# Later expert rows, a longer lag for their second-table products, and fewer of them beside the gate tables

## The chip, the cores and the metric

The kernel runs on one core of a Trainium2 chip. The metric is the device time of one execution in microseconds, less is better; a time is the median of several executions. The engines are named as the profile names them: PE (TensorE, matrix products), DVE (VectorE), ACT (ScalarE), POOL (GpSimd, which here issues the indirect gathers) and SP (which issues plain DMAs).

## What is computed

One decoder layer over 1024 prompt tokens and 8 sample tokens. Three mixers (a state-space scan, a convolution, attention to a memory) are summed and normed; behind them stands a feed-forward step that picks 128 experts for each token out of 16384 (8 heads, 16 each) and costs this case its gathers:

```python
# t: tokens x 1024; idx, gate: tokens x 8 heads x 16 picks, from two top-16 lists of 128 keys
u = jnp.take(u_tab, idx, axis=0)
act = jax.nn.gelu(jnp.einsum('td,thkd->thk', t, u), approximate=False)
v = jnp.take(v_tab, idx, axis=0)
return jnp.einsum('thk,thkd->td', gate * act, v)
# then x <- layer_norm(ALPHA * x + that)
```

Both tables are 16384 x 1024 in float32, so one row of either is 4 KB.

## The kernel before

The prompt is worked in three groups of 256, 384 and 384 tokens, one after the other on PE; the 8 sample tokens ride along. Each group passes the mixers (`front`, `main`), a norm (`norm1`) and the routing, which finds the experts (`routing`, `route`).

**Expert rows.** For the first two groups, five blocks of 128 tokens, the experts are gathered. A "row" is one pick for 128 tokens: one gather of 128 x 4 KB by POOL (`gather`, L442) into one of `UVB` = 8 buffers named `uv`, and the arithmetic on it. In the first table (`block_u`) that is one DVE multiplication whose sum goes into a column of `av` (L455), 128 rows to a block. The second table has two forms. `block_v` gathers strips by `ixt` and lets PE multiply and sum: four rows make a set, and `four(m, vs)` issues the set's eight matmuls (L501). `block_v2` (`second_table`, L544), used once the third group's mixers are done (`strips` is false), gathers by `idx` and does each row with one DVE multiply and add; PE has no part in it. At a block's end stand `layer_norm2` (L436, L439) and the store.

**What sets the pace.** `product`, which every matrix product with a streamed weight calls, first calls `spread`. That adds `pace[0]` (a pair, for first-table and second-table rows) to two counters `due` and issues as many rows as are due. `pace[0]` is taken from `PHASES` in the mixers, from `PACE[-3]` from L1409 on (the third group's norm, its routing and its gate tables), from `PACE[-2]` in the first 24 rounds of the dense loop, and from `PACE[-1]` behind them. The products of a complete set wait in the list `late` until `VLAG` more rows are out, so that the gathers have time to land; a finished block's step to its second table waits there `TLAG` rows.

**What sets the order.** The program text is only the first order. A scheduler then gives each engine its list: of what can be issued it takes the instruction with the lowest number, which is the place in the text. Rows are issued inside `tc.issue_after(last)` (behind the fourth-last DVE instruction that is no row, `LAG`) and `tc.high_priority(-LATER)`, which adds `LATER` to their numbers. The products in `late` get no such number.

**The third group.** Its 384 tokens take no rows: `dense_group` computes all 16384 experts. First, for all tokens, gate tables are made: one-hot products (L1314) go through ACT to tiles `xt` and to DRAM (`gd`, 16 stores, L1321), while 30 of the 128 blocks of activations are computed ahead (`activations`, PE lines L200 and L211) and stored in `ad`. Then `while active` waits for a block of `block_v` in progress, whose last step (L522) reads the accumulators `va`, since the dense loop needs them. The dense loop has 128 rounds: activations of six rounds ahead (read back from `ad` in the first 24, computed behind them), a DVE product with the gates (`weigh`, L1346, tiles read back from `gd`, L1340), and 18 matmuls (L1378). Its layer norms follow (L1382 to L1388), then `while more()` issues the rows that are left, and `sample_final` (L1271, L1272) ends the program. The sample tokens have a state update of their own (L1058 on PE, L1061 on ACT, L1066 to L1075), scheduled between the products of the second group.

Of the kernel before, what the change touches and what calls it, by code (L numbers as in the profile page):

```python
# [37 lines left out]
    ((0, 0),) * 6,  # L38
    ((1.7, 2), (1.8, 1.8), (1.8, 1.8), (2.2, 1.8), (1.4, 1.8), (2.4, 1.8)),
    ((1.4, 2), (1.8, 1.8), (1.8, 1.8), (2.2, 1.8), (1.4, 1.8), (2.4, 1.8))))  # L40
PACE = (1.5, 2.0), (1.0, 1.0), (2.2, 2.2)
LAG = 4
RIDE = 0
LATER = 1000000
PRE = 6
EARLY = 30
STEP = 4
VLAG = 6
TLAG = 10
E2B = 7  # L50
BLKB = 28
# [17 lines left out]
def hybrid_layer(ctx: ExitStack, tc, I, O):  # L69
# [193 lines left out]
    def row(work):  # L263
        while work:
            try:
                next(work[0])
                return
            except StopIteration:
                work.popleft()

    def spread():
# [9 lines left out]
        while max(due) >= 1.0 or (late and not any(tables) and steps < 4):  # L281
# [8 lines left out]
            n = len(nc.cur_bb.bb.instructions)  # L290
            with tc.issue_after(last), tc.high_priority(-LATER):
                row(tables[k])
# [187 lines left out]
    def block_v(g, c, idx, av, avt, ixt):  # L480
# [8 lines left out]
        def four(m, vs):  # L489
            if m == 0:  # L490
                va.extend(pva() for _ in range(2))
            w = slide[m % 2]
            act.activation(w[:, :, 31], avt[:, m:P:32], AF.Copy)

            before = None
            for dh in range(2):
                for j in (3, 0, 1, 2):
                    with ExitStack() as order:
                        if before is not None:
                            order.enter_context(tc.issue_after(before))  # L500
                        before = pe.matmul(va[dh][32 * j:32 * j + 32], w[:, j, 31 - m:63 - m],  # L501
                                           vs[j][:, dh * 512:dh * 512 + 512], start=(m == 0), stop=(m == 31)).ins

        for m in range(32):
            vs = []
            for j in range(4):
# [3 lines left out]
                if j < 3:  # L510
                    yield
            late.append([VLAG, lambda m=m, vs=vs: four(m, vs)])
            yield
        done = []
        late.append([VLAG, lambda: done.append(1)])
        while not done:
# [297 lines left out]
    def norm1(G):  # L814

        g, nt, tb = G.g, G.nt, G.tb
        rs_ = G.rs
        layer_norm_f(rs_, nt)
        for f in range(8):
            act.activation(rs_[f], rs_[f], AF.Identity, scale=col(C_G1, f), bias=col(C_B1, f))  # L820

    def keep_tokens(G):

        for c in range(G.tb):
            for i in range(4):
                pt = psm()
                for f in range(2):
                    pe.transpose(pt[:, f * P:(f + 1) * P], G.rs[2 * i + f][:, c * P:(c + 1) * P], ident)
                xt = blk(256)
                act.activation(xt, pt[:, 0:256], AF.Copy)  # L830
                sp.dma_start(x1d[G.g][c][:, i * 256:(i + 1) * 256], xt)
# [446 lines left out]
    def dense_group(G):  # L1278
# [73 lines left out]
        for c in range(P):  # L1352
            if c + PRE < P:
                if c == 2 * EARLY:
                    keep_tokens(G)
                pace[0] = PACE[-2 if c + PRE < early else -1]
                if c + PRE < early:
# [50 lines left out]
    sp.dma_start(O["state"], hT)  # L1408
    pace[0] = PACE[-3]  # L1409
    norm1(G)  # L1410
# [104 lines left out]
```

## Time and profile before

| | us |
|---|---|
| median of 3 runs (4582.04 to 4594.18) | 4582.82 |
| profiled execution | 4586.19 |
| its span, first to last instruction | 4584.4 |
| PE busy | 3917.6 (85%) |
| DVE busy | 3294.7 (72%) |
| ACT busy | 1755.5 (38%) |
| POOL busy | 1633.8 (36%) |

The third group's routing runs from some 3000 to 3190 us, its gate tables to 3445 us, the dense loop from 3470 to 4540 us, and the tail to 4584.4 us. All rows below are from the profiled execution, whose time is 1.8 us above its span and 3.4 us above the median.

### The profile page before, as it was taken

How to read it: one execution, taken by the hardware profiler on the slowest of the kernel's cores; microseconds unless marked ns; L12 is line 12 of the kernel's file. 1: busy time of each engine (PE TensorE's matmuls, PEld its weight loads, DVE VectorE, ACT ScalarE, POOL GpSimd, SP SyncE). 2: the span in 40 equal slices, each digit the busy share in tenths (PEclk: the TensorE clock that was granted, in tenths of full speed). 3: DMA queues.
4: the chain of work that ended last, by engine and by line, in shares of the span. 5: the costliest groups of instructions: out<-in, count | busy, mean ns of one | idle time of the engine just before them, and what ended most of it. 6: DMA issues, size and time to landing. Idle time of an engine off the chain costs nothing. (4 is left out here: it accounts for less than half of the span.)

```text
span 4584.4 us, 58298 instructions
## 1 busy us (share of the span) xinstructions
PE 3917.6 (85%) x19901; PEld 3043.3 (66%) x19901; DVE 3294.7 (72%) x7235; ACT 1755.5 (38%) x3699; POOL 1633.8 (36%) x1316
## 2 busy tenths in 40 slices
PE   8999898798488888885888888888996999889996
PEld 8888786576377556563666665444664788777895
DVE  4458537775799746776766886458896889888976
ACT  5474243546334314342362322112563333332333
POOL 0000000341422456512444535534322556547631
PEclk9999999898799999997999999999997999999998
DMA  5433344653866899954888879967879999999985
GB/s 173 150 129 132 120 148 155 230 208 110 287 228 225 290 372 344 340 189 144 287 291 317 319 248 332 352 227 258 305 284 321 350 374 389 352 318 295 386 297 188
DMA packets 410041, 1199.41 MB, mean 262 GB/s; under 512 B 42464, under 2 KB 111712, under 8 KB 407568
## 3 DMA queue, kind: packets, MB, share of 16 engines
q0 software_dynamic: 186880, 679.56, 41.7%
q1 hardware_dynamic: 222864, 516.13, 32.4%
q8 instruction: 157, 2.57, 0.2%
q14 instruction: 140, 1.15, 0.1%
HBM read 1141.59 MB, written 53.93 MB: 261 GB/s over the span
## 5 line engine op out<-in xcount | busy, mean ns | idle before, releaser
L442 POOL DMA_INDIRECT uv<-in_peer_u,idx x640 | 794.6, 1242 | 1846.5 <-DVE idx L422 800.9
L200 PE MATMUL mm<-xt,wh 128*128 128x384 f32 (+1 forms) x4224 | 1042.5, 332 | 45.4 <-ACT b L921 28.7
L455 DVE SCALAR_TENSOR_TENSOR uv<-uv,x 128x1024 f32<-128x1024 f32 x640 | 774.0, 1218 | 365.3 <-DMA uv<-in_peer_u,idx 322.8
L200 PEld LDWEIGHTS mm<-xt,wh 128*128 128x128 f32 x4224 | 742.4, 192 | 102.9 <-issue 31.1
L211 PE MATMUL mm<-b,wr 128*128 128x256 f32 (+2 forms) x2304 | 723.5, 466 | 73.6 <-ACT b L737 43.6
L200 PE MATMUL mm<-xt,wl 128*128 128x384 f32 (+1 forms) x2112 | 687.5, 326 | 36.2 <-DVE wl L191 36.0
L189 ACT ACTIVATE wh<-wr 128x1024 fp32r<-128x1024 f32 x362 | 383.1, 1059 | 851.9 <-PE mm L200 371.8
L442 POOL DMA_INDIRECT uv<-in_peer_v,ixt x384 | 437.9, 1140 | 666.8 <-PE va L501 223.8
L211 PEld LDWEIGHTS mm<-b,wr 128*128 128x128 f32 x2304 | 436.2, 195 | 319.2 <-ACT b L737 53.8
L191 DVE TENSOR_TENSOR wl<-wr,wh 128x1024 fp32r<-128x1024 f32 x362 | 441.2, 1219 | 268.4 <-ACT wh L189 263.8
L442 POOL DMA_INDIRECT uv<-in_peer_v,idx x256 | 352.3, 1376 | 340.4 <-DVE uv L544 174.8
L200 PEld LDWEIGHTS mm<-xt,wl 128*128 128x128 f32 x2112 | 404.5, 192 | 51.9 <-DVE wl L191 41.7
L678 DVE SCALAR_TENSOR_TENSOR b<-raw,cc,b 128x384 f32<-128x384 f32 (+1 forms) x720 | 407.2, 568 | 14.8 <-ACT b L676 5.6
L544 DVE SCALAR_TENSOR_TENSOR uv<-uv,av 128x1024 f32<-128x1024 f32 (+1 forms) x269 | 343.4, 1279 | 23.1 <-DMA uv<-in_peer_v,idx 20.1
L501 PE MATMUL va<-uv,slide 128*32 128x512 f32 x1536 | 224.1, 702 | 131.2 <-DMA uv<-in_peer_v,ixt 131.2
L200 PE MATMUL st<-b,wh 128*128 128x384 f32 x784 | 207.5, 347 | 0.5 <-ACT b L830 0.5
L501 PEld LDWEIGHTS va<-uv,slide 128*32 128x32 f32 x1536 | 44.6, 120 | 243.7 <-DMA uv<-in_peer_v,ixt 147.6
L164 ACT ACTIVATE b<-acc 128x384 fp32r<-128x384 f32 x128 | 66.8, 525 | 364.4 <-PE va L1378 256.8
L200 PE MATMUL tp<-b,wh 128*128 128x384 f32 x784 | 203.8, 341 | 0.0
L176 DVE TENSOR_TENSOR wl<-e,wh 128x512 fp32r<-128x512 f32 x256 | 165.1, 682 | 22.9 <-ACT wh L164 22.7
L1378 PE MATMUL mm<-wh,b 128*128 128x512 f32 x512 | 164.8, 403 | 10.0 <-ACT b L164 10.0
L1378 PE MATMUL va<-wh,b 128*128 128x512 f32 x512 | 162.8, 400 | 9.9 <-DVE uv L522 9.9
(408 smaller groups left out, 6371.9 us busy)
## 6 DMA issues: line engine op xcount, KB each, us to landing
wr<-in_win SPq DMA_DIRECT2D x264, 512.0 KB, 4.2
wr<-in_peer_ut SPq DMA_DIRECT2D x128, 512.0 KB, 9.5
e<-in_peer_v SPq DMA_DIRECT2D x256, 256.0 KB, 6.8
wr<-in_wso SPq DMA_DIRECT2D x48, 512.0 KB, 4.4
wr<-in_wq SPq DMA_DIRECT2D x48, 512.0 KB, 5.8
gd<-xt SPq DMA_DIRECT2D x16, 1536.0 KB, 7.5
xt<-gd SPq DMA_DIRECT2D x16, 1536.0 KB, 15.5
wr<-in_wmo SPq DMA_DIRECT2D x24, 512.0 KB, 4.9
```

The costliest lines, as they stand in the source:

```text
L164: act.activation(hi, src, AF.Copy)
L176: dve.tensor_tensor(l, src, f32(h), op=OP.subtract)
L189: act.activation(wh, wr, AF.Copy)
L191: dve.tensor_tensor(wl, wr, f32(wh), op=OP.subtract)
L200: pe.matmul(ps, a[:, k], b[k0 + k], start=(i == 0), stop=(i == n - 1))
L211: pe.matmul(ps, w[:, k], xs[k], start=(k == 0), stop=(k == 7))
L442: pool.indirect_dma_start(out=dst, out_offset=None, in_=table, in_offset=bass.IndirectOffsetOnAxis(ap=idx_col, axis=0))
L455: dve.scalar_tensor_tensor(u, u, 1.0, x1, op0=OP.mult, op1=OP.mult, accum_out=av[:, s:s + 1])
L501: before = pe.matmul(va[dh][32 * j:32 * j + 32], w[:, j, 31 - m:63 - m], vs[j][:, dh * 512:dh * 512 + 512], start=(m == 0), stop=(m == 31) ...
L544: dve.scalar_tensor_tensor(acc, v, av[:, s:s + 1], acc, op0=OP.mult, op1=OP.add)
L678: dve.scalar_tensor_tensor(cv, raw[:, i:i + nt], col(C_FW, j * TAPS + i), cv, op0=OP.mult, op1=OP.add)
L1378: pe.matmul(outs[2 * tbk + dh], a[:, ts], v[:, dh * 512:dh * 512 + 512], start=(c == 0 and i == 0), stop=(c == P - 1 and i == 2))
```

## The change

Three constants move. Rows are numbered 250 places behind their place in the text instead of a million; a set's products and the other entries with `VLAG` wait for eight more rows instead of six; and during the last routing and the gate tables a product makes 0.7 first-table rows due instead of 1.5. No instruction is added or removed; the same rows are computed.

```diff
--- before.py
+++ after.py
@@ -38,14 +38,14 @@
     ((0, 0),) * 6,
     ((1.7, 2), (1.8, 1.8), (1.8, 1.8), (2.2, 1.8), (1.4, 1.8), (2.4, 1.8)),
     ((1.4, 2), (1.8, 1.8), (1.8, 1.8), (2.2, 1.8), (1.4, 1.8), (2.4, 1.8))))
-PACE = (1.5, 2.0), (1.0, 1.0), (2.2, 2.2)
+PACE = (0.7, 2.0), (1.0, 1.0), (2.2, 2.2)
 LAG = 4
 RIDE = 0
-LATER = 1000000
+LATER = 250
 PRE = 6
 EARLY = 30
 STEP = 4
-VLAG = 6
+VLAG = 8
 TLAG = 10
 E2B = 7
 BLKB = 28
```

What becomes of the order shows at three places.

On PE, at some 1165 to 1227 us of the run before, in the second group's mixers: `L1058` is the sample tokens' state update, `L211` and `L200` are matmuls of streamed products, `L691` a sum over channels. Before:

```order
L200 MATMUL mm<-xt,wh 128x384 x2
L200 MATMUL mm<-xt,wl 128x384
L1058 MATMUL st<-ident,proj_s 128x128 x20
L691 MATMUL st<-b,ones 128x384 x8
L1058 MATMUL st<-ident,proj_s 128x128 x4
L211 MATMUL mm<-b,wr 128x384 x8
```

And with the change:

```order
L200 MATMUL mm<-xt,wl 128x384
L1058 MATMUL st<-ident,proj_s 128x128 x4
L211 MATMUL mm<-b,wr 128x384
L1058 MATMUL st<-ident,proj_s 128x128 x4
L211 MATMUL mm<-b,wr 128x384 x7
L200 MATMUL mm<-xt,wh 128x384 x2
L200 MATMUL mm<-xt,wl 128x384
...
L1058 MATMUL st<-ident,proj_s 128x128 x12
L691 MATMUL st<-b,ones 128x384 x8
L1058 MATMUL st<-ident,proj_s 128x128 x4
```

Twenty matmuls of the state update that stood in one run now have eight `L211` and twenty-four `L200` (eight pairs of rows) among them.

On PE, at the passage from the gate tables (`L1314`) to the dense loop (`L1378`); `L501` is a set's product from expert rows into the accumulators `va`. Before:

```order
L1314 MATMUL mm<-e_25612,e_25613 128x128 x2
L1314 MATMUL mm<-e_25648,e_25649 128x128 x4
L1314 MATMUL mm<-e_25661,e_25662 128x128 x4
L1314 MATMUL mm<-e_25674,e_25675 128x128 x4
L501 MATMUL va<-uv,slide_134 32x512 x8
L1378 MATMUL mm<-wh,b 128x512 x2
L1378 MATMUL mm<-wl,b 128x512 x2
L1378 MATMUL ss<-wh,b 128x512
```

And with the change:

```order
L211 MATMUL st<-b,wr 128x384 x7
L1314 MATMUL mm<-e_25504,e_25505 128x128 x4
L1314 MATMUL mm<-e_25517,e_25518 128x128 x4
L1314 MATMUL mm<-e_25530,e_25531 128x128 x4
L1378 MATMUL mm<-wh,b 128x512 x2
L1378 MATMUL mm<-wl,b 128x512 x2
L1378 MATMUL ss<-wh,b 128x512
```

The second-table set that stood last, between tables and loop, is gone from there; it stands earlier, inside the tables.

On DVE, at the end of the program: `L436` and `L439` on `wr` are the dense group's last layer norms, `L544` second-table rows, `L533` the residual of the last gathered block, `L428` its norm, `L1272` the sample tokens' sum. Before:

```order
L544 SCALAR_TENSOR_TENSOR uv<-uv,av 128x1024
L436 SCALAR_TENSOR_TENSOR wr<-wr,ln2d,wl 128x1024
L544 SCALAR_TENSOR_TENSOR uv<-uv,av 128x1024 x3
L439 SCALAR_TENSOR_TENSOR wr<-wr,ln2d,wl 128x1024
L533 SCALAR_TENSOR_TENSOR uv<-uv 128x1024
L428 TENSOR_REDUCE ln2s<-uv 128x1
L1272 SCALAR_TENSOR_TENSOR uv<-uv,st 8x512
```

And with the change:

```order
L436 SCALAR_TENSOR_TENSOR wr<-wr,ln2d,wl 128x1024
L544 SCALAR_TENSOR_TENSOR uv<-uv,av 128x1024 x3
L439 SCALAR_TENSOR_TENSOR wr<-wr,ln2d,wl 128x1024
L544 SCALAR_TENSOR_TENSOR uv<-uv,av 128x1024 x46
L533 SCALAR_TENSOR_TENSOR uv<-uv 128x1024
L428 TENSOR_REDUCE ln2s<-uv 128x1
L1272 SCALAR_TENSOR_TENSOR uv<-uv,st 8x512
```

Forty-six second-table rows stand behind the last dense norm, where none stood; among the dense norms there are six, where there were seven.

Counted in DVE's list, the rows (`L455` and `L544`) in each part are:

| part | before | with the change |
|---|---|---|
| last routing | 27 | 13 |
| gate tables | 23 | 15 |
| from the last table to the first gate product | 8 | 0 |
| rounds c = 0 to 23 | 28 | 26 |
| rounds 24 to 31 | 39 | 22 |
| rounds 32 to 71, each 8 | about 34 | about 34 |
| rounds 72 to 103 in all | 117 | 125 |
| behind the last matmul | 7 | 52 |

## Rows read from the trace of the kernel before

**Rows 1.** Busy time by stretch: columns as the header says, x counts instructions
```profile
core 0: us, PE busy (x) PEld busy (x) DVE busy (x) ACT busy (x) POOL busy (x), PEclk, DMA share, GB/s
1150.00:1240.00 90.00, 30.53 (x96) 22.09 (x95) 68.90 (x248) 28.43 (x70) 40.22 (x30) 0.62 0.85 276
1300.00:1500.00 200.00, 175.05 (x858) 149.38 (x857) 185.03 (x462) 86.54 (x200) 47.23 (x40) 0.92 0.67 222
2824.80:2862.80 38.00, 31.10 (x150) 20.63 (x145) 19.76 (x32) 5.30 (x11) 26.77 (x24) 1.00 1.00 383
3000.00:3190.00 190.00, 167.96 (x659) 84.92 (x658) 135.03 (x633) 32.73 (x75) 76.40 (x73) 0.96 0.76 262
3190.00:3445.00 255.00, 233.80 (x1285) 161.33 (x1285) 235.34 (x767) 151.87 (x137) 73.89 (x61) 0.99 0.79 293
3445.00:3490.00 45.00, 13.99 (x48) 8.15 (x47) 23.28 (x42) 7.99 (x15) 6.95 (x7) 0.62 0.97 335
3616.00:3690.00 74.00, 69.66 (x336) 62.95 (x335) 66.84 (x94) 25.44 (x42) 45.55 (x35) 0.95 1.02 385
4236.00:4540.00 304.00, 302.33 (x1494) 269.81 (x1495) 238.97 (x276) 107.26 (x179) 138.15 (x98) 1.00 0.86 308
4298.00:4347.00 49.00, 49.00 (x249) 44.36 (x248) 47.78 (x53) 16.90 (x29) 35.27 (x24) 1.00 1.04 398
4540.00:4584.40 44.40, 6.69 (x21) 2.98 (x19) 32.97 (x31) 22.20 (x35) 0.00 (x0) 0.59 0.53 179
```

**Rows 2.** What TensorE waited for: total us, times, longest us
```profile
PE va L501 <- DMA uv<-in_peer_v,ixt: 131.2, 46, 11.1
...
PE st L1058 <- ACT sb L1061: 40.6, 5, 19.2
...
PE st L858 <- DVE s_scq L1234: 17.1, 7, 4.3
...
PE va L1378 <- DVE uv L522: 9.9, 1, 9.9
```

**Rows 3.** The same view for GpSimd, which issues the gathers
```profile
POOL uv L442 <- PE va L501: 355.2, 81, 24.8
...
POOL uv L442 <- DVE uv L439: 83.9, 2, 83.2
```

**Rows 4.** Page, part 5: busy, mean ns of one, idle before, releaser
```profile
L200 PE MATMUL mm<-xt,wh 128*128 128x384 f32 (+1 forms) x4224 | 1042.5, 332 | 45.4 <-ACT b L921 28.7
...
L455 DVE SCALAR_TENSOR_TENSOR uv<-uv,x 128x1024 f32<-128x1024 f32 x640 | 774.0, 1218 | 365.3 <-DMA uv<-in_peer_u,idx 322.8
...
L211 PE MATMUL mm<-b,wr 128*128 128x256 f32 (+2 forms) x2304 | 723.5, 466 | 73.6 <-ACT b L737 43.6
...
L544 DVE SCALAR_TENSOR_TENSOR uv<-uv,av 128x1024 f32<-128x1024 f32 (+1 forms) x269 | 343.4, 1279 | 23.1 <-DMA uv<-in_peer_v,idx 20.1
```

**Rows 5.** Page, part 3: the queue of the gathers
```profile
q0 software_dynamic: 186880, 679.56, 41.7%
```

**Rows 6.** Timeline at 1188 us: gathers that start under vector work
```profile
1188.76 1.89 POOL L442 DMA_INDIRECT uv<-in_peer_u,idx  x1 [2.04 <-DVE s_jk L1073]
...
1190.96 1.98 POOL L442 DMA_INDIRECT uv<-in_peer_u,idx  x1 [0.30 <-issue]
```

**Rows 7.** Timeline at 4306 us, GpSimd alone
```profile
4306.90 1.86 POOL L442 DMA_INDIRECT uv<-in_peer_v,idx  x1 [1.12 <-DVE uv L544]
4309.06 1.30 POOL L442 DMA_INDIRECT uv<-in_peer_v,idx  x1 [0.30 <-issue]
```

**Rows 8.** Timeline around the start of the dense loop
```profile
3447.36 0.33 SPq L1321 DMA_DIRECT2D gd<-xt  x1
...
3470.21 1.22 PE L1378 MATMUL mm<-wh,b 128*128 128x512 f32 x2 [9.98 <-ACT b L164]
```

**Rows 9.** Timeline of VectorE after the last dense layer norms
```profile
4563.81 1.28 DVE L439 SCALAR_TENSOR_TENSOR wr<-wr,ln2d,wl 128x1024 f32<-128x1024 f32 x1 [0.23 <-DMA wl<-in_ln]
4565.01 1.22 DVE L533 SCALAR_TENSOR_TENSOR uv<-uv 128x1024 f32<-128x1024 f32 x1
```

## The prediction

> **What bounds the kernel now.** I read the busy times by stretch first, then what PE waited for, then the timeline at the places the waits named. PE is the busiest engine over the span, but it is not the same limit everywhere. The stretches show four kinds of place [rows 1]. In the last rounds of the dense loop (4236 to 4540) PE works 302.33 of 304 us at a granted clock of 1.00: 36 rounds at 8.4 us, and there nothing but PE counts. In the gate tables (3190 to 3445) PE works 233.80 and DVE 235.34 of 255 us: two engines are nearly full, and DVE hands PE its operands. At the passage to the dense loop (3445 to 3490) PE works 13.99 of 45 us at a clock of 0.62: it waits for data. In the tail (4540 to the end) PE has 6.69 us of work in 44.4, POOL none, and what DVE still has to do is the time. So a row costs nothing where it lies beside PE work, something where DVE is nearly full, and its whole length in the tail. The change moves rows out of the second kind of place and into the last.
>
> The waits of PE [rows 2] name what could come free: 131.2 us in 46 waits of the strip products L501 for their gathers, 40.6 us in five waits of the state update L1058 for ACT, 17.1 us at L858, 9.9 us at the loop's first use of `va`.
>
> **The change part by part.** The sum is made against the profiled execution, 4586.19 us, which is 3.4 us above the median; for the median I take 3.4 off at the end.
>
> *The longer lag.* A strip product stalls PE when its gathers have not landed. I went through the 96 sets and counted in POOL's order how many gathers stand between a set's last gather and the first that takes over one of its buffers. Where there were six or more (22 sets) PE waited 6.0 us in all, with five (47 sets) 62.5 us, with four or fewer (27 sets) 62.8 us; together the 131.2 of [rows 2]. With the change the counts are 49, 30 and 17; at the mean wait of each kind, taken block by block since the third block waits less than the second, that makes about 90 us, 41 less. It can be anything from 0 to 41 on the path, because a wait that goes lets PE run into the next one. I take 19 ahead of 3000 us, about half, and leave the rest to the stages below. The lag also holds a set's four buffers longer: behind it the next gathers queue on POOL, which already waits 355.2 us for L501 [rows 3]. POOL has spare time there, so I cost that at nothing; where it isn't spare, it takes back part of the 19.
>
> *The earlier rows, ahead of 3000 us.* Three places. At 1150 to 1240 us PE works 30.53 of 90 us [rows 1] and L1058 waits for ACT. With the change, eight L211 and twenty-four L200 stand among its matmuls instead of outside: 8 x 0.466 + 24 x 0.332 [rows 4] = 11.7 us of work goes into the wait, so -12, at least 0. At 2112 us a gather waited 83.2 us for L439, a block's last norm [rows 3]; the norm now stands behind its own first half, and the next block's gathers come sooner. PE had other work in that time, so I take -4 (0 to -8, the length of one strip product's wait). Against that, first-table rows run up to ten ahead of before between 1350 and 1900 us, and at 1300 to 1500 DVE works 185.03 of 200 us [rows 1]: ten rows of 1.218 us [rows 4] and the sum's read-out come to 13 us; part lies in the 15 us that are free: +9 (0 to +13). Together -26.
>
> *The last routing, 3000 to 3190.* Its DVE list has 14 rows fewer, 14 x 1.3 = 18 us of DVE. PE is idle 22 us there, 17.1 of it at L858 for a DVE result [rows 1, 2]. A row in front of that result is up to 1.2 us each time and there are seven waits: I take -10 (0 to -18).
>
> *The gate tables.* Eight rows fewer, 10.4 us of DVE, which is as full as PE; PE is idle 21 us. -12 with the last strip set, which no longer stands behind the tables (0 to -21).
>
> *The passage.* The last store of gate tables goes out at 3447.36 and the loop's first matmul starts at 3470.21 [rows 8]; between them lie the store, its reading back, and gathers at a DMA share of 0.97 [rows 1]. With the change no row of DVE and few gathers stand there, the wait for `va` (9.9 us) goes, and so does the last strip set. PE's idle 31 us are the bound; what stays is the round trip through DRAM. I take -18 (0 to -31).
>
> *The clock.* The passage's 13.99 us of PE at 0.62 would be 8.7 at full clock, -5; the 30.53 us at 1150 would be 18.9, -12. Both stretches keep most of their gaps. I take -5 (0 to -17).
>
> *Dense rounds.* In rounds 24 to 31 (3616 to 3690) 17 rows go; the stretch takes 74 us against 8 x 8.4 = 67 us in the last rounds, DVE works 66.84 and the DMA share is 1.02 [rows 1]: -7, and no more than that. In rounds 72 to 103 eight rows come; beside PE they cost between 0 and 10 us: +5. In the other rounds nothing moves.
>
> *The tail.* 45 more rows than before, behind the last dense norm, where at 4563.81 and 4565.01 DVE goes straight from that norm to the residual [rows 9]; POOL has nothing to do there now. No work hides them: 45 times the time of a row. The floor is DVE, 1.279 us [rows 4]: 58 us. DMA: 679.56 MB in rows of 0.524 MB are 1296, and 41.7% of 4584.4 us over them is 1.475 us each [rows 5]: 66 us. The best that 24 gathers in a row did is 38.0 / 24 = 1.58 us, at a DMA share of 1.00 (2824.8 to 2862.8) [rows 1]: 71 us. The slow end: a gather that starts under a vector operation with two tensors in SBUF takes 1.86 to 1.98 us, and the next starts 0.30 later [rows 6, 7]; 49 us at 4298 hold 24 gathers, 2.04 us each [rows 1]; at 1.89 + 0.30 = 2.2 us it is 99. I take 1.58, because DVE has nothing else in the tail and a row that waits for its gather leaves POOL free: +71 (58 to 99).
>
> The sum: -26 - 10 - 12 - 18 - 5 - 7 + 5 + 71 = -2. That gives 4584 profiled, **4581 us** for the median.
>
> The Trainium skill has a rule that speaks against this tail: "SBUF — State Buffer", section "Who interferes with whom", says that a VectorE instruction with two SBUF inputs contends with a GpSimd instruction that reads SBUF, and that whichever issues first holds the shared pair for its whole length while the other fully blocks. By that, a row's vector work and its gather's issue would add up, 1.28 + 0.94 = 2.2 us, the slow end above. The trace agrees in one direction: gathers take 1.86 to 1.98 us when they start under such an operation [rows 6, 7].
>
> **The rivals.**
>
> *The tail runs at the slow end.* Mechanism: each gather starts just as the DVE row that freed its buffer is followed by the next row, so it waits that row out. For it: the pairs at 4306 us [rows 7], where exactly that happens. Against it: there DVE was full with the dense loop's own work (47.78 of 49 us [rows 1]). 45 x 2.2 = 99, 28 more than I took: 4609, slower. The gains ahead come to 73 net of the +5, so the change breaks even at 1.62 us a row and is measurably slower from 1.93 us.
>
> *PE takes over in routing, tables and passage.* If the rows are what holds these three, their idle 22 + 21 + 31 = 74 us goes whole instead of the 40 taken, and with it the low clock of the passage: some -40 more, 4541. For it: PE and DVE are equally full in the tables. Against it: the waits named there that a row can have caused are 17.1 and 9.9 [rows 2].
>
> *The rows were covered.* The rows taken out lie beside work that was going on anyway: the routing is held by its own chain, the passage by the trip through DRAM. Then half of the 40 comes and nothing of the clock: +25, 4606. So the change doesn't bring what its fewer rows promise, and the tail is paid in full.
>
> **How the numbers follow.** A difference under 0.3%, 13.7 us, can't be told from none here. The forecast, gains and tail about equal, has 0.44 and its own range 4556 to 4603: 0.14 of it lies below 4569, 0.24 within, 0.06 above. PE taking over 0.28 (0.26 faster, 0.02 within). The slow tail 0.17 (0.15 slower, 0.02 within) and covered rows 0.11 (0.10, 0.01). Faster 0.40, same 0.29, slower 0.31. The range reaches from beyond the second rival (4541, and 21 for the L501 and clock terms at their ends: 4520) to slow tail with part of the covered rows: 4628.
>
> **What would show it.** A tail of some 115 us after the last dense matmul instead of 44, with 45 L544 at 1.5 to 1.6 us each, says the tail term is right; 2.2 us says the first rival. The stretch from the last L1314 to the first L1378 should be shorter, without L501 or L522 in it, L858's waits under 10 us, L501's near 90 and L1058's near 29. I am wrong if the tables don't get shorter with their rows gone, or if the stretch up to 3000 us, where most of the time lies, moves by more than the 26 us I gave it: there the order of the rows changes nearly everywhere, and I costed three places of it.

## The result

The changed kernel took 4732.54 us (4705.3 to 4739.38, 4 runs) against 4588.5 us (4582.04 to 4595.66, 4 runs) of the kernel before: a ratio of 1.0299, 95% interval 1.0271 to 1.0326. It is slower by 3%, some 143 us, and outside the range of the prediction. Its profiled execution has a span of 4727.7 us, 143.3 more than before.

Setting the same PE matmul of both traces side by side (the n-th of its line), the span falls into seven stretches. The first row of the forecast holds the lag's -19 as well:

| stretch | before, us | after, us | difference | forecast |
|---|---|---|---|---|
| up to the last matmul of the sample tokens' mixer (L1215) | 2994.0 | 3062.9 | +68.9 | -26 |
| from there to the first gate-table matmul (last routing) | 196.1 | 179.7 | -16.4 | -10 |
| gate tables, first to last L1314 | 255.1 | 265.6 | +10.5 | -12 |
| passage, to the first L1378 into `va` | 43.4 | 23.6 | -19.8 | -18 |
| dense rounds 0 to 71 | 580.0 | 583.4 | +3.4 | -7 |
| dense rounds 72 to the last matmul | 474.9 | 508.2 | +33.3 | +5 |
| tail | 40.9 | 104.3 | +63.4 | +71 |

The forecast had another -5 for the clock; the mean granted clock fell instead, from 0.933 to 0.923.

The busy times of the changed kernel by stretch, to be set beside [rows 1]: last routing, tables, passage, rounds 24 to 31, the sample tokens' rounds 80 to 95, and the tail. Columns are as there.

```profile
core 0: us, PE busy (x) PEld busy (x) DVE busy (x) ACT busy (x) POOL busy (x), PEclk, DMA share, GB/s
3069.00:3242.50 173.50, 161.13 (x636) 83.18 (x636) 120.62 (x608) 32.55 (x74) 55.18 (x54) 0.97 0.70 237
3242.50:3508.00 265.50, 242.24 (x1324) 166.49 (x1323) 232.16 (x755) 158.64 (x152) 62.61 (x56) 0.99 0.76 271
3508.00:3533.00 25.00, 7.13 (x22) 5.26 (x21) 8.73 (x17) 4.78 (x8) 0.94 (x1) 0.59 0.92 295
3658.40:3725.10 66.70, 66.70 (x338) 60.42 (x336) 53.54 (x80) 24.41 (x40) 30.00 (x21) 1.00 0.86 292
4193.00:4376.30 183.30, 151.86 (x674) 132.32 (x674) 135.06 (x169) 54.77 (x89) 97.19 (x65) 0.91 0.93 264
4620.20:4727.70 107.50, 6.39 (x20) 2.74 (x18) 90.98 (x76) 22.20 (x35) 48.04 (x45) 0.54 0.78 294
```

The tail is the clearest. It is 107.5 us long against 44.4, DVE works 90.98 of it instead of 32.97 us, and POOL, which had nothing to do, works 48.04 us on 45 gathers. In the passage PE idles 18 us instead of 31, and rounds 24 to 31 run with PE full. The tables grew although eight rows are gone from them: two strip sets more are multiplied there (176 matmuls of L501 instead of 144), and PE is busy 8.4 us longer there. The sample tokens' rounds (4193 to 4376.3) leave PE 31 us idle at a clock of 0.91.

What PE waited for, beside [rows 2] (total us, times, longest), then POOL, beside [rows 3]:

```profile
PE va L501 <- DMA uv<-in_peer_v,ixt: 103.7, 38, 6.2
...
PE st L1058 <- ACT sb L1061: 49.3, 6, 23.4
...
PE mm L1378 <- ACT b L164: 17.9, 1, 17.9
...
PE st L858 <- DVE s_scq L1234: 8.0, 6, 3.1
```

```profile
POOL uv L442 <- PE va L501: 388.0, 68, 22.2
...
POOL uv L442 <- DVE uv L439: 34.7, 2, 31.2
```

L501 waits 27.5 us less, L858 9.1 less, and the wait for `va` is gone; the loop's first matmul still waits, 17.9 us, for the gate tables' trip through DRAM. L1058 waits 8.7 us more. POOL waits 33 us more for L501 and 49 less for L439. The longer lag is not what makes POOL wait: with the lag alone it waits 296.5 us for L501, with the nearer rows alone 489.2. So most waits that were forecast to shrink shrank; the time went where no term of size had been set.

### The profile page after: what moved, and what is told of

It reads as the page before. It is cut to its first block, busy times and chain, and to the rows that moved or that the text cites. A ratio compares the mean times of both kernels' runs of the same rounds, so it can differ in the third digit from the quotient of the medians.

```text
span 4727.7 us, 58367 instructions
## 1 busy us (share of the span) xinstructions
PE 3948.9 (84%) x19901; PEld 3062.6 (65%) x19901; DVE 3304.5 (70%) x7235; ACT 1748.1 (37%) x3694; POOL 1586.5 (34%) x1316
## 3 DMA queue, kind: packets, MB, share of 16 engines
q0 software_dynamic: 186880, 679.56, 40.9%
## 5 line engine op out<-in xcount | busy, mean ns | idle before, releaser
L442 POOL DMA_INDIRECT uv<-in_peer_u,idx x640 | 763.7, 1193 | 2102.2 <-DVE idx L422 856.8
L455 DVE SCALAR_TENSOR_TENSOR uv<-uv,x 128x1024 f32<-128x1024 f32 x640 | 775.4, 1221 | 433.7 <-DMA uv<-in_peer_u,idx 354.5
L200 PE MATMUL mm<-xt,wh 128*128 128x384 f32 (+1 forms) x4224 | 1040.7, 332 | 44.0 <-ACT b L921 27.5
L200 PEld LDWEIGHTS mm<-xt,wh 128*128 128x128 f32 x4224 | 744.2, 192 | 99.8 <-issue 30.7
L211 PE MATMUL mm<-b,wr 128*128 128x256 f32 (+2 forms) x2304 | 729.4, 469 | 77.6 <-ACT b L737 38.7
L200 PE MATMUL mm<-xt,wl 128*128 128x384 f32 (+1 forms) x2112 | 691.4, 328 | 38.1 <-DVE wl L191 37.5
L211 PEld LDWEIGHTS mm<-b,wr 128*128 128x128 f32 x2304 | 438.9, 196 | 334.0 <-issue 54.3
L200 PEld LDWEIGHTS mm<-xt,wl 128*128 128x128 f32 x2112 | 405.2, 192 | 55.9 <-DVE wl L191 44.0
L678 DVE SCALAR_TENSOR_TENSOR b<-raw,cc,b 128x384 f32<-128x384 f32 (+1 forms) x720 | 408.8, 571 | 17.9 <-ACT b L676 8.1
L544 DVE SCALAR_TENSOR_TENSOR uv<-uv,av 128x1024 f32<-128x1024 f32 (+1 forms) x269 | 344.0, 1280 | 28.7 <-DMA uv<-in_peer_v,idx 18.6
L501 PE MATMUL va<-uv,slide 128*32 128x512 f32 x1536 | 216.7, 688 | 103.7 <-DMA uv<-in_peer_v,ixt 103.7
L200 PE MATMUL tp<-b,wh 128*128 128x384 f32 x784 | 209.2, 349 | 0.5 <-ACT wh L189 0.5
L200 PE MATMUL st<-b,wh 128*128 128x384 f32 x784 | 207.3, 346 | 0.5 <-ACT b L830 0.5
L1378 PE MATMUL mm<-wh,b 128*128 128x512 f32 x512 | 164.4, 402 | 19.3 <-ACT b L164 17.9
L501 PEld LDWEIGHTS va<-uv,slide 128*32 128x32 f32 x1536 | 43.5, 118 | 208.6 <-DMA uv<-in_peer_v,ixt 117.7
L164 ACT ACTIVATE wh<-e 128x512 fp32r<-128x512 f32 x256 | 148.3, 624 | 58.8 <-PE va L1378 52.2
```

Of the source, the lines that this page charges most:

```text
L164: act.activation(hi, src, AF.Copy)
L200: pe.matmul(ps, a[:, k], b[k0 + k], start=(i == 0), stop=(i == n - 1))
L211: pe.matmul(ps, w[:, k], xs[k], start=(k == 0), stop=(k == 7))
L442: pool.indirect_dma_start(out=dst, out_offset=None, in_=table, in_offset=bass.IndirectOffsetOnAxis(ap=idx_col, axis=0))
L455: dve.scalar_tensor_tensor(u, u, 1.0, x1, op0=OP.mult, op1=OP.mult, accum_out=av[:, s:s + 1])
L544: dve.scalar_tensor_tensor(acc, v, av[:, s:s + 1], acc, op0=OP.mult, op1=OP.add)
```

## The experiments

Times are compared within each group of runs, since chips differ: the unchanged kernel's median was 4588.5, 4605.46, 4596.45 and 4599.08 us in the four groups. Single profiled executions with the same list of instructions up to there drift apart by up to 39 us over 3000 us (by 12 at most up to 1520 us), so only larger steps, or steps inside one stretch, are read from one trace.

### One constant at a time

```diff
-PACE = (1.5, 2.0), (1.0, 1.0), (2.2, 2.2)
+PACE = (0.7, 2.0), (1.0, 1.0), (2.2, 2.2)
```

> Only the pace pair of the last routing and the gate tables goes from 1.5 to 0.7; rows keep their million, the lag its six. Theory (each constant has its own place of loss): nothing moves up to 3000 us, so the 69 us that the changed kernel is behind at 2990 us are absent; the routing is 10 to 16 us shorter, the passage shorter, but the sample tokens' rows fall into later dense rounds (80 to 104) and cost about 40 us there, and the tail is 104 us long instead of 41. Sum about +60 to +80: 4645 to 4665. Rival (the dense loss comes from rows being placed nearer to their place in the text, not from the pace): the dense rounds lose nothing, +30 to +45: 4615 to 4630.

Measured: 4662.97 us, ratio 1.0121 (1.0074 to 1.0168).

```diff
-LATER = 1000000
+LATER = 250
```

> Only the place of the rows in the scheduler's list moves, from a million behind to 250; pace 1.5, lag six. Theory: rows of the first table come earlier in DVE's list at 1300 to 1560 us and at 1790 to 1830 us, where DVE is nearly full, and PE waits behind them: about +45 by 1830 us, held to the end; the tail is as long as before (7 rows): +30 to +60, 4615 to 4645. Rival (the loss ahead of 3000 us is that of the longer lag, which holds the gather buffers longer): within 15 us of the kernel before.

Measured: 4669.05 us, ratio 1.0158 (1.0103 to 1.0212).

```diff
-VLAG = 6
+VLAG = 8
```

> Only the lag of the strip products goes from six to eight rows; pace 1.5, rows a million behind. Theory: the waits of the strip products for their gathers fall from 131 to about 100 us, most of it is taken back by other waits, and the time moves by -20 to +5: 4565 to 4590. Rival (buffers held longer make the gathers late): GpSimd's wait for the strip products grows by 30 us and more, and the kernel is 30 to 60 us slower, most of it ahead of 3000 us.

Measured: 4639.67 us, ratio 1.0074 (1.0052 to 1.0096).

```diff
-LATER = 1000000
+LATER = 250
-VLAG = 6
+VLAG = 8
```

> The changed kernel with its pace put back to 1.5: rows 250 behind, lag eight. Theory: the sum of the two alone, +40 to +70 (4625 to 4655), all of it in place at 3000 us; tail of 9 rows as before. Rival (the two make up for each other, a shorter distance in the list and a longer lag): within 15 us of the kernel before, so that the pace alone makes the whole loss.

Measured: 4688.54 us, ratio 1.0186 (1.0139 to 1.0233).

All three constants lose by themselves, 1.2, 1.6 and 0.7%, together 3.5% against the 3.0% of the whole. None makes up for another. The nearer rows cost more than their theory had, alone (4645 at most) and with the lag (4655). For the lag both sides were partly wrong. It is slower, which the theory had not, and PE's wait for the gathers of L501 did not fall to 100 us but is 143.4. The rival had the size; but POOL's wait for L501 did not grow, 296.5 us against the 355.2 of [rows 3], and ahead of 2300 us nothing moved.

The stretches of each trace, with the unchanged kernel from the third group (its expectation first; the other four are from the second, on another chip):

> The kernel before, unchanged, with a profile on the chip of these runs, so that its stretches can be set against those of the others on one chip. Every theory expects its usual time there, 4580 to 4620, and the same shape: tail 41 us, dense loop slowest where the sample tokens' rows are.

Measured: 4580.25 us.

| | to L1215 | routing | tables | passage | rounds 0-71 | rounds 72- | tail, to PE's and DVE's last |
|---|---|---|---|---|---|---|---|
| unchanged | 3001.3 | 189.6 | 251.9 | 43.6 | 576.0 | 475.2 | 37.9 |
| pace alone | 3032.5 | 172.6 | 257.2 | 22.8 | 588.8 | 496.3 | 103.7 |
| 250 alone | 3049.5 | 195.9 | 283.7 | 27.0 | 593.8 | 469.7 | 37.8 |
| lag alone | 3016.1 | 207.5 | 260.0 | 60.2 | 570.4 | 482.5 | 39.4 |
| 250 and lag | 3055.0 | 211.7 | 280.3 | 26.8 | 590.2 | 470.4 | 38.9 |

(The last column ends with the last instruction of an engine, some 3 us ahead of the span's end.) The tail belongs to the pace: 103.7 against 37.9 us. So does the shorter routing. The 250 costs 48 us ahead of L1215 and 32 in the tables; of the 48, drift can be a large part. The lag costs in routing, where PE's wait at L858 for DVE is 28.3 us against 12.8 and 17.1 in the two traces of the unchanged kernel, and at the passage, where two strip sets are left behind the tables instead of one. There a strip product of the last gathered block comes to stand inside the dense loop; PE in the trace with the lag alone, its wait in brackets:

```profile
3533.57 3.64 PE L501 MATMUL va<-uv,slide 128*32 128x512 f32 x16 [16.02 <-DMA uv<-in_peer_v,ixt]
...
3543.81 0.80 PE L1378 MATMUL va<-wh,b 128*128 128x512 f32 x1 [6.59 <-DVE uv L522]
```

PE waits 16.02 us for gathers, and another 6.59 for `va`, where the loop had begun already. With the pace of 0.7 the block is done ahead of the passage, and that loss can't occur; the lag was undone inside the change to see that:

```diff
-VLAG = 8
+VLAG = 6
```

> The changed kernel with its lag put back from eight rows to six: pace 0.7, rows 250 behind. Theory: the lag alone lost 0.7%, two thirds of it in routing and at the passage to the dense loop, where with the lower pace the last strip set stands well ahead; so undoing it here brings less, 5 to 15 us: a ratio of 1.026 to 1.029. Rival (its cost is the same everywhere): 30 to 35 us, a ratio of 1.021 to 1.024.

Measured: 4721.85 us, ratio 1.0254 (1.0232 to 1.0276). Against the 1.0299 of the changed kernel (1.0271 to 1.0326) that is 0.45%, less than the 0.74 of the lag alone. The ratio lies between those of theory and rival, and its interval reaches into both, so the two are not told apart. The stretches agree within 5 us in every place but the routing, 173.7 against 179.7 us.

### Where the nearer rows lose

The two halves of `LATER = 250`, split where the third group's mixers end:

```diff
-            with tc.issue_after(last), tc.high_priority(-LATER):
+            with tc.issue_after(last), tc.high_priority(-(LATER if strips[0] else 1000000)):
```

> Rows stand 250 places behind only until the third group's mixers end; behind that a million again; pace 1.5, lag six. Theory (what costs is rows put earlier among vector work that fills DVE, at 1150 to 1540 us): the 45 us that the run with 250 throughout had lost by 1540 us are lost again, the 25 to 30 it lost in routing and gate tables are not: +35 to +50. Rival (the loss by 1540 us is made good later, and only that in the tables lasts): within 15 us of the kernel before.

Measured: 4636.45 us, ratio 1.0066 (1.0036 to 1.0095). Of the 58.8 us between the profiled spans 53.5 are there at L1215 (3054.8 against 3001.3), and every stretch behind it is within 5 us of the unchanged one; the timed runs, with drift evened out, make it 30 us (17 to 44).

```diff
-            with tc.issue_after(last), tc.high_priority(-LATER):
+            with tc.issue_after(last), tc.high_priority(-(1000000 if strips[0] else LATER)):
```

> The other half: a million until the third group's mixers end, 250 places behind from there on; pace 1.5, lag six. Theory: nothing moves up to 3000 us; 31 rows stand beside the gate tables and their first gate products where DVE is as full as PE, and cost 25 to 30 us there; the dense loop gives back 5 to 10: a ratio of 1.003 to 1.006. Rival: the loss of the run with 250 throughout came ahead of 3000 us alone, then within 0.2% of the kernel before.

Measured: 4629.05 us, ratio 1.0057 (1.004 to 1.0074). The tables take 281.3 instead of 251.9 us; the passage gives 18 back, rounds 0 to 71 take 20 more. The two halves add to 1.23%, against 1.58% for the whole (1.03 to 2.12). What PE waits for in the tables is the next one-hot factor from DVE (L1312), here in the unchanged kernel and then in this one:

```profile
PE mm L1314 <- DVE e L1312: 1.1, 2, 0.6
```

```profile
PE mm L1314 <- DVE e L1312: 13.6, 11, 4.5
```

DVE has 29 rows in its list there, where it had 23, and these stand ahead of work that PE needs instead of behind it. That is 12.5 of the 29 us. For the rest PE waits 6.4 us more for strip gathers and is busy 10.6 us longer, with a set more and at a granted clock of 0.95 instead of 0.99. To see whether the loss grows with the nearness, the first half was run with no distance at all:

```diff
-LATER = 250
+LATER = 0
```

> As the run with rows 250 places behind until the third group's mixers end, but with 0 places there: a row competes with the work of its own place in the text. Theory (a row put ahead of the chain of vector work delays it, so the loss grows as rows come nearer to their place): clearly more than the 0.7% of the run with 250, a ratio of 1.012 to 1.03, with the added loss where DVE is fullest, 1150 to 1560 us. Rival (the loss is one of a single stretch that happens to fall badly, not of the distance): 1.004 to 1.009 again.

Measured: 4712.87 us, ratio 1.0232 (1.0202 to 1.0261), against 1.0066 with 250. Where the time goes shows when the same matmuls are set side by side again (times of the unchanged kernel of the third group, differences to it). Up to 1638 us five traces with the old order of rows, six with 250 and the one with 0 lie clearly apart:

| piece of the same work | old order | 250 (changed kernel) | 0 |
|---|---|---|---|
| 1131 to 1474 us | -4 to 0 | +12 to +20 (+11.5) | +56 |
| 1474 to 1518 us | -1 to 0 | +23 to +28 (+27.8) | +20 |
| 1518 to 1638 us | -2 to +4 | -8 to -17 (-16.6) | -8 |

In all 23 to 37 us are lost with 250 by 1638 us. From there to L1215 it is 11 to 36 more, against -5 to 24 in the old order, which drift can make; at distance 0 it is 73, not taken apart here.

*The first piece.* At its end, 8 rows more than in the old order are done with 250, and 15 more with 0: at 1.3 us a row on DVE, with the sum's read-out, 10 and 20 us. Do the rows also hold DVE up by waiting for gathers that have not landed? DVE's wait at L455 and PE's at L768 (the attention's normed weights), over this piece in the unchanged kernel and at distance 0:

```profile
DVE uv L455 <- DMA uv<-in_peer_u,idx: 6.4, 3, 2.8
...
PE tp L771 <- DVE b L768: 4.2, 3, 2.7
```

```profile
DVE uv L455 <- DMA uv<-in_peer_u,idx: 10.0, 7, 2.3
...
PE tp L771 <- DVE b L768: 18.0, 6, 8.0
```

Hardly: at distance 0 the waits for gathers are 3.6 us longer, and in the changed kernel they are 5.5 us, no longer than in the unchanged one. What makes PE wait is the rows' own work. The longest wait at distance 0, PE and then DVE:

```profile
1390.88 0.66 PE L771 MATMUL tp<-ident,b 128*128 128x128 f32 x2 [8.03 <-DVE b L768]
```

```profile
1382.55 1.21 DVE L455 SCALAR_TENSOR_TENSOR uv<-uv,x 128x1024 f32<-128x1024 f32 x1
...
1389.24 1.22 DVE L455 SCALAR_TENSOR_TENSOR uv<-uv,x 128x1024 f32<-128x1024 f32 x1
...
1390.38 0.35 DVE L768 TENSOR_SCALAR b<-b,att 128x256 f32<-128x256 f32 x1
```

Five rows stand between 1382.55 and 1390.38, DVE is at work all through, and none of them waits for its gather. With a million, rows stand behind such work. What else makes the 56 us at distance 0 is not shown.

*The second piece.* In the unchanged kernel, and the same work in the changed one (columns as above):

```profile
1473.80:1517.70 43.90, 42.25 (x209) 34.55 (x208) 42.54 (x80) 16.01 (x25) 8.79 (x8) 1.00 0.61 201
1488.40:1560.20 71.80, 58.58 (x271) 40.68 (x270) 53.67 (x99) 15.17 (x26) 29.30 (x27) 0.88 0.75 262
```

The rows that run ahead end their block sooner, so its strip products start sooner. Four sets (64 matmuls of L501) stand in this piece now, where PE was full and had none. They take PE some 10 us, PE waits 10.3 us for their gathers, and the granted clock is 0.88 instead of 1.00. In the third piece, where the sets come from, 8 to 17 us are given back.

### Where the later rows go

```diff
-PACE = (0.7, 2.0), (1.0, 1.0), (2.2, 2.2)
+PACE = (0.7, 2.0), (2.5, 2.5), (2.2, 2.2)
```

> The changed kernel, with the pace of the first 24 dense rounds raised from 1.0 to 2.5, so that 16 rows are left behind the last matmul instead of 52. Theory (rows in the tail cost 1.46 us each, beside the dense loop less): the tail is 53 us shorter, rounds 24 to 31 have some 60 rows instead of 24 and cost 15 to 25 us more; in all 25 to 45 us faster than the changed kernel, a ratio of 1.020 to 1.025 to the kernel before. Rival (the dense loop pays for a row as much as the tail does): the tail is as much shorter, the dense loop as much longer, ratio 1.03 as with the changed kernel.

Measured: 4705.84 us, ratio 1.0232 (1.0208 to 1.0256). The tail falls from 101.5 to 51.6 us (to the last instruction of an engine), rounds 72 to the end from 508.2 to 474.3, and rounds 0 to 71 grow from 583.4 to 642.8: 84 us are saved at one end of the loop and in the tail, 59 spent at the other. Rounds 24 to 31 hold 58 rows and take 12.53 us each instead of 8.34. In the timed runs that is 0.7% of gain, as the theory had it. So a row beside the dense loop is not free where the rounds are already full.

Two kernels then looked for the room that is left, with rows a million behind and a lag of six:

```diff
-PACE = (1.5, 2.0), (1.0, 1.0), (2.2, 2.2)
+PACE = (1.0, 2.0), (2.0, 2.0), (2.2, 2.4)
```

> The kernel before (a million, lag six) with other paces: 1.0 in routing and gate tables instead of 1.5, 2.0 in the first 24 dense rounds instead of 1.0, 2.2 and 2.4 behind them; no row is left behind the last matmul. Theory (fewer rows beside routing and tables are worth something once they don't go to the tail): 10 to 30 us faster than the kernel before, a ratio of 0.993 to 0.998, of which 9 to 12 in the tail. Rival (rows cost the dense loop what they save ahead of it): within 5 us.

Measured: 4563.14 us, ratio 0.9934 (0.9907 to 0.996).

```diff
-PACE = (1.5, 2.0), (1.0, 1.0), (2.2, 2.2)
+PACE = (1.1, 2.0), (1.0, 1.0), (1.98, 1.98)
...
                 pace[0] = PACE[-2 if c + PRE < early else -1]
+                if not tables[0]:
+                    pace[0] = 0.0, 4.4
```

> A million and lag six as before, other paces: 1.1 beside routing and gate tables, 1.0 in the first 24 dense rounds, 1.98 in each of the others, and 4.4 for second-table rows once the first table's list is empty. Theory (in the dense loop DVE has room for about four rows in a round of 8.4 us; the 4.4 of before overfill the rounds in which both lists have rows, and 2.2 leave room unused at the end): rounds with 32 rows in 8 run at 8.4 to 8.9 us instead of 9.3, no row is left for the tail, and the time is 40 to 70 us under the kernel before, a ratio of 0.985 to 0.991. Rival (the middle rounds are held by DMA traffic, not by the number of vector rows): 0.992 to 0.996, as the run with paces 1.0, 2.0 and 2.2.

Measured: 4551.41 us, ratio 0.9908 (0.9881 to 0.9936): faster than both kernels. The time alone does not exclude the rival (0.992 to 0.996); the rounds do, for some of them. Rounds 64 to 71 and 104 to 111 and the tail in its trace (columns as above):

```profile
3981.40:4048.30 66.90, 66.90 (x337) 60.46 (x336) 64.62 (x89) 24.43 (x40) 44.47 (x33) 1.00 1.03 393
4344.50:4411.40 66.90, 66.90 (x337) 60.44 (x336) 66.14 (x73) 24.15 (x40) 47.87 (x33) 1.00 1.04 399
4513.50:4541.70 28.20, 6.07 (x18) 2.45 (x17) 19.56 (x20) 17.70 (x28) 0.00 (x0) 0.65 0.61 204
```

Both groups of eight rounds hold 32 rows and take 66.9 us, 8.36 each, with PE full and DVE at 65 to 66 of 66.9 us. In the kernel before, rounds 24 to 63 with 33 to 36 rows to the eight took 8.4 to 11.0 us, 9.6 in the mean. About four rows a round is what DVE carries beside its own work; the rows over that are paid by PE, and the rounds from 104 on had room for 14 more in each eight that no one used. The rival's DMA limit is not needed for these groups: they move rows at a DMA share of 1.0 and run at PE's pace. It can't be excluded for rounds with more rows, where both DVE and DMA are full. Not every round follows. Rounds 56 to 63 take 11 us in all these kernels; they hold work that the others have not, the 24 transposes of `keep_tokens` at round 60 (L828), at which PE waits 6.2 us for ACT in the kernel before and 13.5 in this one. The rounds with the sample tokens' rows take some 10 us in this one too.

## Why the prediction was wrong

**The step that failed is "the earlier rows, ahead of 3000 us", with the lag's -19 that was summed with it.** I priced three places and the lag there and summed them to -26; the profiled stretch lost 69, the largest piece of the 151 us between forecast and result (4581 and 4732). Some of the 69 is drift between executions; the timed runs give 30 us to the nearer rows there and 34 to the lag, which acts for the most part behind it. Two errors sit in the rows' term, +9. Their own length on DVE, 13 us at most, came about as costed: 11.5 us by 1474. But I overlooked that rows that run ahead bring the strip sets of their block ahead too, into a stretch where PE was full, which cost 28 us more, of which 17 came back by 1638. And I read the order at the places that looked worth a gain, and took all else as unchanged, though the order of the rows had moved nearly everywhere. I had written that down as what would make the forecast wrong.

**L1058, -12, was nothing.** The products did move into the wait. PE in the changed kernel at that place:

```profile
1172.69 2.08 PE L1058 MATMUL st<-ident,proj_s 128*128 128x128 f32 x8 [23.38 <-ACT sb L1061]
...
1217.59 2.07 PE L1058 MATMUL st<-ident,proj_s 128*128 128x128 f32 x8 [17.05 <-ACT sb L1061]
1220.62 4.60 PE L691 MATMUL st<-b,ones 128*128 128x384 f32 x7 [0.95 <-ACT sb L1061]
```

The waits are 23.38 and 17.05 us where they were 15.41 and 19.21, and L691 behind them starts at 1220.62, 4 us later than before (3 of them were there at 1131). So the chain of the state update, for whose ACT step (L1061) PE waits there, sets the end of that stretch; work that is put into its gaps only leaves the place where it stood before. A wait of PE is a gain only if PE's own work ends the stretch.

**The longer lag, -19, cost 0.7%.** L501's waits went to 103.7 us, near the 90 I had worked out, but not by the lag. Up to L1215 they are 104.3 us before and 103.7 in the changed kernel; with the lag alone they are 111.1, with the lag put back to six inside the change 98.8. So counting the gathers between a set and the reuse of its buffers did not forecast the waits; why is open. What went are the 26.9 us of the last gathered block behind L1215, and the lower pace takes those away: with the lag at six they are 1.1 us. That the end of a block gets longer (the last set and the entry behind it each stand eight rows in `late` instead of six) was not seen, and with the pace of 1.5 it reaches into the dense loop.

**The tables, -12, went to +10.5.** With the pace alone they are 257.2 us, with 250 and its 29 rows 280 to 284, with both 265.6. At a million, fewer rows gained nothing, since PE hardly waited for DVE's factors there (1.1 us). The strip sets that left the routing and the passage were not costed: with the pace alone one set more stands in the tables and PE is busy 4.7 us longer, in the changed kernel it is two sets and 8.4 us, where the tables grew by 10.5.

**Routing -10, passage -18, rounds 24 to 31 -7** came as -16.4, -19.8 and -7.3. There the waits named at the place were what ended the stretch.

**Rounds 72 to 103, +5, took 33.** I costed eight rows at about half a microsecond each. The first table's last block ends later, so the rounds in which both lists have rows, 4.4 a round, reach to round 96 instead of 86 (the last gather of a sample row starts at 4378 us, before at 4222), and those rounds are slow: 88 to 95 take 11.6 us each with 35 rows, before 8.7 with 32. The number of rows alone does not explain that, since rounds 72 to 79 take 9.7 with 34. One piece of the changed kernel's trace (POOL, DVE, PE):

```profile
4238.62 8.57 POOL L442 DMA_INDIRECT uv<-in_peer_v,idx  x1 [3.23 <-DVE uv L553]
...
4252.58 1.22 DVE L553 SCALAR_TENSOR_TENSOR uv<-uv 64x1024 f32<-64x1024 f32 x1 [6.22 <-DMA uv<-in_peer_u,s_idx]
...
4256.66 0.69 PE L200 MATMUL tp<-b,wl 128*128 128x384 f32 x1 [5.25 <-DVE wl L191]
```

DVE stands 6.22 us at a sample row (L553) whose gather hasn't landed, behind a gather that held POOL for 8.57 us; the dense loop's own work stands behind that row, and PE waits 5.25 us. That the pace does this is shown (the pace alone takes 21 us more there, and with 250 alone these rounds get shorter). How much of the 33 us these waits make, and why POOL takes 6 to 12 us for single gathers there, is not settled.

**The tail, +71, was +63.** The mechanism and the place were right, and the first rival, with 2.2 us a row, was wrong. DVE in the changed kernel's tail, then POOL:

```profile
4644.49 1.29 DVE L439 SCALAR_TENSOR_TENSOR wr<-wr,ln2d,wl 128x1024 f32<-128x1024 f32 x1 [1.08 <-DMA wl<-in_ln]
4645.71 58.07 DVE L544 SCALAR_TENSOR_TENSOR uv<-uv,av 128x1024 f32<-128x1024 f32 x44
4704.58 1.28 DVE L544 SCALAR_TENSOR_TENSOR uv<-uv,av 128x1024 f32<-128x1024 f32 x1 [0.80 <-DMA uv<-in_peer_v,idx]
```

```profile
4658.66 1.02 POOL L442 DMA_INDIRECT uv<-in_peer_v,idx  x1 [0.30 <-issue]
4659.99 1.01 POOL L442 DMA_INDIRECT uv<-in_peer_v,idx  x1 [0.30 <-issue]
```

Forty-four rows take 58.07 us, 1.32 each, and with the ends of the stretch 63.4 / 45 = 1.41. Each gather takes 1.02 us and the next one starts 0.30 behind it: 1.32 again. POOL falls into step with DVE, starting each gather as a row ends (at 4658.66, and DVE's next row at 4658.90), and pays almost nothing for it. I had weighed a rule of the Trainium skill, "SBUF — State Buffer", section "Who interferes with whom", by which a VectorE instruction with two SBUF inputs and a GpSimd instruction that reads SBUF block each other for their whole length. In this tail the two run side by side at 1.32 us a row, where blocking each other would need 1.28 + 0.94 us: the trace does not bear out the full block for these gathers.

**The rivals.** "PE takes over" came nearest in the passage, where PE still idles 18 of the 31 us, and was wrong for the tables. "The rows were covered" was right for the tables. The loss ahead of 3000 us was in none of them.

## What to carry to other kernels

A term that moves work in an in-order queue is priced by what it then stands ahead of, and by what its earlier end sets off elsewhere (here the strip products on PE), not by its length alone. Here background rows were best behind everything else: a million places behind beat 250, and 250 beat 0 where both were run. Where an edit changes the order over the whole program, price the stretches by their length, and give those that were not looked at a range of their own. Background work spread over a loop has a capacity per round (here some four rows): find the rounds that are over it and those with room, and level them, before moving work into a stretch where nothing covers it.

## What the runs showed that was not expected

In the tail, vector rows and gathers run at 1.32 us a row in step, though gathers that start in the middle of a row take 1.86 to 1.98 us [rows 6]. Single gathers held POOL for 6.18, 8.57 and 12.34 us in and just behind the changed kernel's rounds with sample rows, with 64-row gathers among the 128-row ones; but one of 9.17 us stands at 3522 us with 250 alone, ahead of all 64-row gathers. And the same kernel differs by chip and execution more than the three runs of before showed: its executions lay between 4580 and 4624 us over the four groups.
